# A decoder trunk on one core: gate and up in two passes over a chunk, and the matrices moved to multiples of 512 bytes

## The chip, the cores and the metric

The kernel runs on one core of a Trainium2 chip. The metric is the time of one execution on the device in microseconds (us), smaller is better. All times below are of the kernel before the change, and the trace is of one execution of it.

## What is computed

Two layers of a decoder trunk on a sequence of 256 positions and a width of 1024, all in float32. Each layer has a mixer part and a feed-forward part:

```
for l in range(DEPTH):                      # 2 layers
    h = rms_norm(x, attn_norm[l])
    proj = h @ w_in[l]                      # retention, sparse attention and gMLP heads
    mix = concatenate([retention(...), nsa(...), spatial_gating(...)])
    x = x + mix @ w_out[l]
    h = rms_norm(x, ffn_norm[l])
    gate, up = split(h @ w_gate_up[l], 2)   # 1024 -> 2 x 2816
    x = x + (silu(gate) * up) @ w_down[l]   # 2816 -> 1024
```

## The kernel before

**Three products for one.** Every matrix that meets a weight is split into a high and a low part, both of type float32r: the weights into `whi` and `wlo`, the activations into `hh` and `hl` (side by side in one tile, `hcat`, seen whole as `hx`). A product is then hh·whi + hl·whi + hh·wlo.

**The stream of weights.** The weights come in pieces of at most 128 x 1024 floats. A piece lands in one of three staging tiles `wst` (a DMA from SyncE's queue), ScalarE casts it to one of six tiles `whi` (CAST), VectorE subtracts to one of six tiles `wlo` (TENSOR_TENSOR). A staging tile comes free when its low part is made; `done` gives `whi` and `wlo` back when the piece has been used. `split_hi[i]` and `ready[i]` are the events that say that the high and the low part of piece i exist.

**Three ways of multiplying.** A matmul has a stationary operand, 128 columns that are loaded into TensorE, and a moving one that streams past it.
- `project` (the mixer's input chunks and the first chunk of gate and up): the activation is stationary, the weights move. A chunk is 8 blocks of the inner dimension (k) x 2 row tiles x 3 products = 48 matmuls. Per layer five mixer chunks and the first chunk of gate and up have 512 columns, one has 384 and one, `nv`, has 274.
- `project_t` (the other ten chunks of gate and up in each layer): the weights are stationary, the activations move. Per chunk 8 k x 4 column groups, each with a wide matmul of 512 columns (whi with hh and hl together) and a narrow one of 256 (wlo with hh). The four results are in four PSUM banks, two of `acc` and two of `sm`.
- `residual` (the output projection with 8 k, the down projection with 22): the activation is stationary (`ah`, `al`, `nsh`, `rth`, ...), the weights move, 4 parts x 3 products of 512 columns per k. In the very last call one of the four parts is cut into two of 256 columns.

**What sets the order.** A planner (`Desk.run`) with costs of its own writes out one fixed order for each engine when the program is built; on the chip an engine takes its instructions in that order and waits for semaphores. Nearly every instruction is issued from one line of a helper, L201, so the rows below are told apart by the tiles' names.

**Where the tiles lie.** Tiles are laid one behind the other in a partition's memory, each in whole slots of 32 bytes. The first tile of the kernel starts at byte 16512, which is 128 past a multiple of 512. All tiles up to `hcat` have sizes that are multiples of 512 bytes, so `wst`, `whi`, `wlo`, `x` and `hcat` all start 128 past. Then come tiles of odd sizes, so that the pools opened later (`ah`, `al`, `nsh`, `nsl`, `gmh`, `gml`, `rth`, `rtl`, `Q`, `Kh`, `Kl`) start 288 past a multiple of 512. A stationary operand of 128 float32r columns takes 512 bytes in a partition.

Of the kernel before, what the change touches and what calls it, by code (L numbers as in the profile page):

```python
# [10 lines left out]
F32R = mybir.dt.float32r  # L11
# [6 lines left out]
T = 256  # L18
# [133 lines left out]

START = [(0, 0), (1, 0), "w", "w", (0, 1), (1, 1), "w", "w"]

NR, NREP = 33, 3
# [238 lines left out]
class Trunk:  # L396
    def __init__(self, ctx, tc, x, wts, cst, oh, relb, par, w1, w2, wsT, out):
        self.ctx, self.tc, self.nc = ctx, tc, tc.nc
        nc = self.nc
        self.d = dict(x=x, wts=wts, cst=cst, oh=oh, relb=relb, par=par, w1=w1, w2=w2, wsT=wsT, out=out)  # L400
        self.PE, self.V = Engine("PE", nc.tensor), Engine("DVE", nc.vector)
        self.A, self.G = Engine("ACT", nc.scalar), Engine("POOL", nc.gpsimd)
        self.SP, self.GQ = Engine("DMA", nc.sync), Engine("SWDMA", nc.gpsimd)

        def preload(table):
            if table == "lnexp":
                nc.scalar.preload_act_table_set("natural_log_exp_and_others")

        self.desk = Desk(preload)
        self.keep = ctx.enter_context(tc.tile_pool(name="keep", bufs=1))  # L410
        psum = ctx.enter_context(tc.tile_pool(name="psum", bufs=1, space=bass.MemoryType.PSUM))
        bank = lambda n: psum.tile([128, 512], F32, tag=n, name=n)
        self.acc = Pool([bank(f"acc{i}") for i in range(4)])
        self.sm = Pool([bank(f"sm{i}") for i in range(4)])
        self.norms = 0
        self.wst = Pool([self.fixed(f"wst{i}", [128, 1024]) for i in range(3)])
        self.whi = Pool([self.fixed(f"whi{i}", [128, 1024], F32R) for i in range(6)])
        self.wlo = Pool([self.fixed(f"wlo{i}", [128, 1024], F32R) for i in range(6)])
        self.w2k = Pool([self.fixed(f"w2k{i}", [128, 512]) for i in range(6)])
# [12 lines left out]
        self.extra = []  # L432

    def fixed(self, name, shape, dt=F32):
        return self.keep.tile(shape, dt, tag=name, name=name)

    def tiny(self, name, shape, dt=F32):
        if name not in self.tinies:
# [74 lines left out]
    def weights(self, i, a):  # L513
        return self.part(self.hi, i, a), self.part(self.lo, i, a)

    def done(self, i):
        self.desk.give(self.whi, self.hi.pop(i))
        self.desk.give(self.wlo, self.lo.pop(i))

    def mm3(self, ps, a, w, first, last):  # L520

# [5 lines left out]

    def setup(self):
        nc = self.nc
        c = self.fixed("cst", [128, C_W])  # L530
        self.cst = c
        self.ident = c[:, C_ID : C_ID + 128]
        self.tri = c[:, C_TRI : C_TRI + 128]
        self.rowvalid = c[:, C_RV : C_RV + 1]
        self.vmask = c[:96, C_VM : C_VM + 6]
        self.dec = c[:, C_DEC:].rearrange("p (h n) -> p h n", h=6)
        self.kc = self.fixed("kc", [128, 2, 2, 16], F32R)
        self.B = self.fixed("B", [128, 6, 256])
        self.Bc = self.fixed("Bc", [128, 2, 3, 2, 16])
        self.par = self.fixed("par", [128, P_W])  # L540
        self.qg = self.fixed("qg", [128, 1])
        self.wsT = self.fixed("wsT", [128, 4, 128])
        self.w1 = self.fixed("w1", [128, 2, 16, 64])
        self.w2 = self.fixed("w2", [128, 64])
        self.ev_cst, self.ev_bias, self.ev_scr = Event(), Event(), Event()
        self.ev_par = [Event() for _ in range(L)]
        self.ev_lay = [Event() for _ in range(L)]
        self.ev_cmp = [Event() for _ in range(L)]
        self.ev_dec = Event()
        self.ev_w = [Event() for s in START if s == "w"]  # L550
        self.ev_sent = [Event() for s in START if s == "w"]
        self.ev_x = [[Event(), Event()] for _ in range(2)]
# [459 lines left out]
    def compress(self, l):  # L1012
# [43 lines left out]

        pk = yield Need(self.sm)
        yield PE.matmul(pk[:32, :64], hk, self.w2[:64, :], start=True, stop=True)
        sq, ss = tiny("csq", [32, 64]), tiny("css", [32, 1])
        yield A.activation(sq, pk[:32, :64], AF.Square, accum_out=ss)  # L1060
        yield V.tensor_scalar(ss, ss, 1.0 / 64, EPS, op0=ALU.mult, op1=ALU.add)
        r = yield from self.rsqrt(ss, "crs")
        kd = tiny("kd", [32, 2, 64])
        yield [V.tensor_scalar_mul(kd[:, i, :], pk[:32, :64], r) for i in range(2)]
        give(self.sm, pk)
        pt = yield Need(self.sm)
# [319 lines left out]
    def mix_open(self, l):  # L1386
        pool = self.tc.tile_pool(name=f"mix{l}", bufs=1, reuse_waits="tile")
        mix = pool.__enter__()

        def tl(name, shape, dt=F32):  # L1390
            return mix.tile(shape, dt, tag=name, name=f"{name}_{l}")

        self.gmh, self.gml = tl("gmh", [128, 2, 256], F32R), tl("gml", [128, 2, 256], F32R)
        self.nsh = [tl(f"nsh{j}", [128, 256], F32R) for j in range(3)]
        self.nsl = [tl(f"nsl{j}", [128, 256], F32R) for j in range(3)]
        self.rth, self.rtl = tl("rth", [128, 3, 256], F32R), tl("rtl", [128, 3, 256], F32R)
        self.Q = tl("Q", [128, 6, 256], F32R)
        self.Kh, self.Kl = (tl(k, [128, 2, 2, 256], F32R) for k in ("Kh", "Kl"))
        self.aT = tl("aT", [128, 2, 272])
# [7 lines left out]
        self.S = Pool([tl(f"S{i}", [128, 512]) for i in range(NS)])  # L1407
        pair = lambda: [Event(), Event()]
# [79 lines left out]
    def project_t(self, pieces, then):  # L1488


        mm = self.PE.matmul
        ps = []
        for j in range(4):
            p = yield Need(self.acc if j < 2 else self.sm)
            ps.append(p)
        for i in pieces:
            yield self.ready[i]
            for a in range(2):
                k = 2 * (i - pieces[0]) + a
                for t in range(2):  # L1500
                    yield self.hready[t][k]
                wh, wl = self.weights(i, a)
                cols = [slice(j * 128, j * 128 + 128) for j in range(4)]
                last = k == KD - 1
                wide = [
                    mm(ps[j], wh[:, s], self.hx[:, k].rearrange("p r n -> p (r n)"), start=k == 0, stop=last, lat=False)
                    for j, s in enumerate(cols)
                ]
                low = [
                    mm(ps[j][:, :T], wl[:, s], self.hh[:, k, :], start=False, stop=False, lat=False)  # L1510
                    for j, s in enumerate(cols)
                ]
                for op in low + wide if last else wide + low:
                    yield op
            self.done(i)
        self.desk.after = self.desk.LAT["PE"]
        then(ps)
        self.desk.after = 0
# [127 lines left out]
    def main(self):  # L1646
# [13 lines left out]
        for l in range(L):  # L1660
# [50 lines left out]
                after = self.store  # L1711
            yield from self.residual(l, idx("down")[0], KF, 3, 4, acted, True, after, l + 1 == L)
            pool.__exit__(None, None, None)


def trunk_kernel(tc, *args):
# [51 lines left out]
```

## Time and profile before

| | |
|---|---|
| median of 3 runs | 637.78 us (637.48 to 637.89) |
| the profiled execution's own time | 638.01 us |
| its span in the trace | 636.2 us (1.8 us lie around it) |
| TensorE (PE) matmuls, busy | 630.5 us |
| VectorE (DVE) busy | 448.5 us |
| ScalarE (ACT) busy | 365.8 us |
| DMA traffic | 111.63 MB, mean 175 GB/s |
| granted TensorE clock | 1.0, the 2.4 GHz level, in all 40 slices |

A row of the trace gives a matmul a duration that runs from its start to the modelled end of its result, so durations of neighbouring matmuls overlap. What a matmul costs is the distance from its start to the start of the next one; it is read from the start column of the timeline.

### The profile page before, as it was taken

How to read it: one execution, taken by the hardware profiler on the slowest of the kernel's cores; microseconds unless marked ns; L12 is line 12 of the kernel's file. 1: busy time of each engine (PE TensorE's matmuls, PEld its weight loads, DVE VectorE, ACT ScalarE, POOL GpSimd, SP SyncE). 2: the span in 40 equal slices, each digit the busy share in tenths (PEclk: the TensorE clock that was granted, in tenths of full speed). 3: DMA queues.
4: the chain of work that ended last, by engine and by line, in shares of the span. 5: the costliest groups of instructions: out<-in, count | busy, mean ns of one | idle time of the engine just before them, and what ended most of it. 6: DMA issues, size and time to landing. Idle time of an engine off the chain costs nothing.

```text
span 636.2 us, 9911 instructions
## 1 busy us (share of the span) xinstructions
PE 630.5 (99%) x3638; PEld 534.7 (84%) x3638; DVE 448.5 (70%) x970; ACT 365.8 (57%) x679; POOL 10.7 (2%) x25
## 2 busy tenths in 40 slices
PE   8999999999999999999999999999999999999997
PEld 6888788888888888888888988888888888888886
DVE  4989996586667767654488898866857767766432
ACT  5869844675555555543377795546755555555330
POOL 1120000000000000100000000000000000000000
PEclk9999999999999999999999999999999999999999
DMA  8974153356555555575436522625565555565631
GB/s 308 305 270 161 31 178 124 114 185 214 187 191 186 183 198 183 189 266 193 133 134 227 176 90 71 203 100 165 189 199 181 193 195 171 191 196 173 201 101 66
DMA packets 33600, 111.63 MB, mean 175 GB/s; under 512 B 4291, under 2 KB 5571, under 8 KB 33552
## 3 DMA queue, kind: packets, MB, share of 16 engines
q1 hardware_dynamic: 33232, 110.62, 52.8%
q8 instruction: 28, 0.46, 0.3%
q0 software_dynamic: 176, 0.36, 0.1%
q14 instruction: 20, 0.16, 0.1%
q10 hardware_dynamic: 144, 0.03, 0.0%
HBM read 109.64 MB, written 1.35 MB: 174 GB/s over the span
## 4 chain that ended last, share of the span: by engine, by line
PE 98%; DMA 1%; DVE 0%; SPq 0%; issue 0%; ACT 0%
PE acc L201 69%; PE sm L201 29%; DMA wst<-in_wts_dram 1%; SPq L201 0%; DVE S L201 0%; DVE x L201 0%; ACT hcat L201 0%; DVE amx L201 0%; ACT whi L201 0%
## 5 line engine op out<-in xcount | busy, mean ns | idle before, releaser
L201 DVE TENSOR_TENSOR wlo<-wst,whi 128x1024 fp32r<-128x1024 f32 (+3 forms) x196 | 234.0, 1197 | 131.6 <-ACT whi L201 130.6
L201 ACT CAST whi<-wst 128x1024 fp32r<-128x1024 f32 (+3 forms) x196 | 200.7, 1028 | 183.7 <-PE sm L201 49.6
L201 PE MATMUL acc<-whi,hcat 128*128 128x512 f32 (+2 forms) x512 | 139.4, 379 | 0.3 <-ACT hcat L201 0.3
L201 PEld LDWEIGHTS acc<-whi,hcat 128*128 128x128 f32 x512 | 91.0, 188 | 15.3 <-ACT whi L201 0.6
L201 PE MATMUL acc<-hcat,whi 128*128 128x512 f32 x320 | 101.2, 396 | 0.0
L201 PE MATMUL sm<-hcat,whi 128*128 128x512 f32 x320 | 99.7, 392 | 0.0
L201 PE MATMUL acc<-wlo,hcat 128*128 128x512 f32 (+2 forms) x256 | 79.5, 378 | 0.0
L201 PEld LDWEIGHTS sm<-hcat,whi 128*128 128x128 f32 x320 | 59.9, 188 | 14.2
L201 PEld LDWEIGHTS acc<-hcat,wlo 128*128 128x128 f32 x320 | 58.8, 188 | 11.8
L201 PE MATMUL sm<-hcat,wlo 128*128 128x256 f32 x320 | 64.0, 281 | 0.0
L201 PE MATMUL acc<-hcat,wlo 128*128 128x256 f32 x320 | 63.8, 281 | 0.0
L201 PEld LDWEIGHTS acc<-hcat,whi 128*128 128x128 f32 x320 | 50.9, 190 | 1.7
L201 PEld LDWEIGHTS acc<-wlo,hcat 128*128 128x128 f32 x256 | 46.4, 188 | 6.9
L201 PE MATMUL acc<-whi,ah 128*128 128x512 f32 (+1 forms) x176 | 50.7, 382 | 0.0
L201 PE MATMUL acc<-whi,al 128*128 128x512 f32 (+1 forms) x176 | 50.6, 381 | 0.0
L201 PE MATMUL acc<-wlo,ah 128*128 128x512 f32 (+1 forms) x176 | 50.4, 380 | 0.0
L201 PEld LDWEIGHTS sm<-hcat,wlo 128*128 128x128 f32 x320 | 49.5, 190 | 0.0
L201 PEld LDWEIGHTS acc<-whi,al 128*128 128x128 f32 x176 | 31.8, 188 | 6.2
L201 PEld LDWEIGHTS acc<-wlo,ah 128*128 128x128 f32 x176 | 31.8, 188 | 6.2
L201 PEld LDWEIGHTS acc<-whi,ah 128*128 128x128 f32 x176 | 31.9, 188 | 6.1
L201 ACT ACTIVATE hcat<-sm,par 128x128 fp32r<-128x128 f32 (+1 forms) x56 | 17.3, 393 | 10.1 <-PE sm L201 9.8
L201 DVE SCALAR_TENSOR_TENSOR hcat<-sm,par,hcat 128x128 fp32r<-128x128 f32 (+1 forms) x56 | 17.4, 362 | 6.0 <-ACT hcat L201 6.0
(213 smaller groups left out, 732.6 us busy)
## 6 DMA issues: line engine op xcount, KB each, us to landing
wst<-in_wts_dram SPq DMA_DIRECT2D x179, 512.0 KB, 3.5
PT<-in_wts_dram SPq DMA_DIRECT2D x7, 512.0 KB, 7.6
wst<-in_wts_dram SPq DMA_DIRECT2D x8, 384.0 KB, 3.1
w<-in_w_dram SPq DMA_DIRECT2D x4, 512.0 KB, 7.7
wst<-in_wts_dram SPq DMA_DIRECT2D x3, 411.0 KB, 4.1
x<-in_x_dram SPq DMA_DIRECT2D x4, 256.0 KB, 5.0
wst<-in_wts_dram SPq DMA_DIRECT2D x4, 256.0 KB, 4.1
B<-scr SPq DMA_DIRECT2D x4, 192.0 KB, 3.7
```

The costliest lines, as they stand in the source:

```text
L201: return Op(self.name, lambda: fn(*a, **k), dur, table, lat, prio, banks)
```

## The change

`project_t` goes over a chunk twice: first all wide products with `whi` (it waits for `split_hi` of a piece), then all narrow products with `wlo` (it waits for `ready`). `done` is cut in two: a high part goes back to its pool once its wide products are issued and its low part exists, a low part once its narrow products are issued. All other code paths issue the same operations as before.

The second part moves tiles. A tile `pad` ahead of `wst` (384 bytes) makes the first matrix start at byte 16896, a multiple of 512; the tiles made in `setup` are put in an order in which the large ones keep to multiples of 512; a second pad does the same for the pools of each layer; `aT`, whose size is no multiple of 512, goes behind the others. `csq`, a small scratch tile, is dropped and `kd` used in its place. In the built program `wst`, `whi`, `wlo`, `x`, `hcat`, `ah`, `al`, `nsh`, `nsl`, `gmh`, `gml`, `rth`, `rtl`, `Q`, `Kh`, `Kl` all start at a multiple of 512. No tile changes its size or its type.

```
+FIRST, SLOT, GRAIN = 16512, 32, 512
...
+        self.kept = 0
+        self.pad(FIRST)
         self.wst = Pool([self.fixed(f"wst{i}", [128, 1024]) for i in range(3)])
...
     def fixed(self, name, shape, dt=F32):
+        size = 4
+        for n in shape[1:]:
+            size *= n
+        self.kept += -(-size // SLOT) * SLOT
         return self.keep.tile(shape, dt, tag=name, name=name)
+
+    def pad(self, first):
+        gap = -(first + self.kept) % GRAIN
+        if gap:
+            self.fixed(f"pad{self.kept}", [128, gap // 4])
...
+    def done_hi(self, i):
+        def release():
+            yield self.ready[i]
+            self.desk.give(self.whi, self.hi.pop(i))
+        self.desk.fork(release())
+
+    def done_lo(self, i):
+        self.desk.give(self.wlo, self.lo.pop(i))
...
     def project_t(self, pieces, then):
...
-        for i in pieces:
-            yield self.ready[i]
-            for a in range(2):
-                k = 2 * (i - pieces[0]) + a
-                for t in range(2):
-                    yield self.hready[t][k]
-                wh, wl = self.weights(i, a)
-                cols = [slice(j * 128, j * 128 + 128) for j in range(4)]
-                last = k == KD - 1
-                wide = [
-                    mm(ps[j], wh[:, s], self.hx[:, k].rearrange("p r n -> p (r n)"), start=k == 0, stop=last, lat=False)
-                    for j, s in enumerate(cols)
-                ]
-                low = [
-                    mm(ps[j][:, :T], wl[:, s], self.hh[:, k, :], start=False, stop=False, lat=False)
-                    for j, s in enumerate(cols)
-                ]
-                for op in low + wide if last else wide + low:
-                    yield op
-            self.done(i)
+        cols = [slice(j * 128, j * 128 + 128) for j in range(4)]
+        for i in pieces:
+            yield self.split_hi[i]
+            for a in range(2):
+                k = 2 * (i - pieces[0]) + a
+                for t in range(2):
+                    yield self.hready[t][k]
+                wh = self.part(self.hi, i, a)
+                for j, s in enumerate(cols):
+                    yield mm(
+                        ps[j], wh[:, s], self.hx[:, k].rearrange("p r n -> p (r n)"), start=k == 0, stop=False, lat=False
+                    )
+            self.done_hi(i)
         for i in pieces:
             yield self.ready[i]
             for a in range(2):
                 k = 2 * (i - pieces[0]) + a
+                wl = self.part(self.lo, i, a)
+                for j, s in enumerate(cols):
+                    yield mm(ps[j][:, :T], wl[:, s], self.hh[:, k, :], start=False, stop=k == KD - 1, lat=False)
+            self.done_lo(i)
...
+        self.pad(FIRST)
```

In the program before, TensorE has in a chunk of gate and up, at its first k (`acc` and `sm` are PSUM banks, `hcat` the moving activations, `whi` and `wlo` the stationary weights; the last number is the columns that move):

```order
L201 MATMUL acc_63<-hcat,whi_75 128x512
L201 MATMUL acc_64<-hcat,whi_75 128x512
L201 MATMUL sm_68<-hcat,whi_75 128x512
L201 MATMUL sm_67<-hcat,whi_75 128x512
L201 MATMUL acc_63<-hcat,wlo_81 128x256
L201 MATMUL acc_64<-hcat,wlo_81 128x256
L201 MATMUL sm_68<-hcat,wlo_81 128x256
L201 MATMUL sm_67<-hcat,wlo_81 128x256
```

Wide and narrow change every four matmuls, eight times in a chunk. In the changed program the one place in a chunk where they change, at the last k of the wide ones and the first of the narrow ones:

```order
L203 MATMUL acc_63<-hcat,whi_78 128x512
L203 MATMUL acc_64<-hcat,whi_78 128x512
L203 MATMUL sm_68<-hcat,whi_78 128x512
L203 MATMUL sm_67<-hcat,whi_78 128x512
L203 MATMUL acc_63<-hcat,wlo_81 128x256
L203 MATMUL acc_64<-hcat,wlo_81 128x256
L203 MATMUL sm_68<-hcat,wlo_81 128x256
L203 MATMUL sm_67<-hcat,wlo_81 128x256
```

Here 32 wide matmuls stand ahead of this place and 32 narrow ones from it on; the order of the k and of the column groups is as before.

VectorE makes the low parts and takes in the results of a chunk (`w2k<-acc`, `w2k<-sm`, the product with `rbc`, the product of gate and up, `al`). Before, around the end of one chunk:

```order
L201 TENSOR_TENSOR wlo_83<-wst_72,whi_77 128x1024
L201 TENSOR_TENSOR w2k_87<-acc_63,w2k_87 128x256
L201 TENSOR_TENSOR wlo_84<-wst_73,whi_78 128x1024
L201 TENSOR_TENSOR w2k_87<-acc_64,w2k_87 128x256
L201 TENSOR_TENSOR w2k_87<-w2k_87,rbc_1486 128x512
L201 TENSOR_TENSOR wlo_85<-wst_71,whi_79 128x1024
L201 TENSOR_TENSOR w2k_89<-sm_68,w2k_89 128x256
L201 TENSOR_TENSOR wlo_80<-wst_72,whi_74 128x1024
L201 TENSOR_TENSOR w2k_89<-sm_67,w2k_89 128x256
L201 TENSOR_TENSOR w2k_89<-w2k_89,w2k_87 128x512
L201 TENSOR_TENSOR wlo_81<-wst_73,whi_75 128x1024
```

In the changed program, around the end of one chunk:

```order
L203 TENSOR_TENSOR wlo_82<-wst_74,whi_76 128x1024
L203 TENSOR_TENSOR wlo_83<-wst_72,whi_77 128x1024
L203 TENSOR_TENSOR w2k_88<-acc_63,w2k_88 128x256
L203 TENSOR_TENSOR w2k_88<-acc_64,w2k_88 128x256
L203 TENSOR_TENSOR w2k_88<-w2k_88,rbc_1486 128x512
L203 TENSOR_TENSOR wlo_84<-wst_73,whi_78 128x1024
L203 TENSOR_TENSOR w2k_90<-sm_68,w2k_90 128x256
L203 TENSOR_TENSOR w2k_90<-sm_67,w2k_90 128x256
L203 TENSOR_TENSOR w2k_90<-w2k_90,w2k_88 128x512
L203 TENSOR_TENSOR wlo_85<-wst_74,whi_79 128x1024
L203 TENSOR_TENSOR al_3_1478<-w2k_90,ah_3_1467 128x512
```

The subtractions stood one by one between the additions; now the two additions of a pair stand together, and per chunk it is still four subtractions beside the same seven other operations. ScalarE's order changes in the same way within the chunks of gate and up; outside them the orders of VectorE, ScalarE and TensorE are the same as before.

## Rows read from the trace of the kernel before

**Rows 1.** The page: busy time of the engines, the granted clock, and the chain that ended last.

```profile
PE 630.5 (99%) x3638; PEld 534.7 (84%) x3638; DVE 448.5 (70%) x970; ACT 365.8 (57%) x679; POOL 10.7 (2%) x25
...
PEclk9999999999999999999999999999999999999999
...
PE 98%; DMA 1%; DVE 0%; SPq 0%; issue 0%; ACT 0%
```

**Rows 2.** What TensorE waited for in the whole span: us in total, times, longest.

```profile
PE sm L201 <- DVE w2k L201: 1.4, 1, 1.4
PE sm L201 <- DMA x<-in_x_dram: 0.5, 1, 0.5
PE acc L201 <- ACT hcat L201: 0.3, 1, 0.3
PE sm L201 <- DVE amx L201: 0.2, 1, 0.2
```

**Rows 3.** Timeline of TensorE in a mixer chunk of `project`, 512 columns, stationary `hcat` (128 past a multiple of 512): start, length of the merged row, instruction, count.

```profile
36.06 1.07 PE L201 MATMUL acc<-whi,hcat 128*128 128x512 f32 x4
36.97 0.62 PE L201 MATMUL acc<-wlo,hcat 128*128 128x512 f32 x2
37.42 1.07 PE L201 MATMUL acc<-whi,hcat 128*128 128x512 f32 x4
38.33 0.62 PE L201 MATMUL acc<-wlo,hcat 128*128 128x512 f32 x2
38.78 1.07 PE L201 MATMUL acc<-whi,hcat 128*128 128x512 f32 x4
```

**Rows 4.** The same view in the down projection of the first layer, 512 columns, stationary `ah` and `al` (288 past a multiple of 512).

```profile
302.74 1.09 PE L201 MATMUL acc<-wlo,ah 128*128 128x512 f32 x4
303.67 1.09 PE L201 MATMUL acc<-whi,al 128*128 128x512 f32 x4
304.60 1.10 PE L201 MATMUL acc<-whi,ah 128*128 128x512 f32 x4
305.54 1.09 PE L201 MATMUL acc<-wlo,ah 128*128 128x512 f32 x4
```

**Rows 5.** The same view in `project_t`, one chunk of gate and up from its start (203.74) to the start of the next (214.95); stationary `whi` and `wlo` (128 past). Rows of two stand in turn on `acc` and `sm`; those left out are the second pair of a four, and from 213.06 to 214.02 eight narrow ones follow each other.

```profile
203.74 0.62 PE L201 MATMUL acc<-hcat,whi 128*128 128x512 f32 x2
...
204.65 0.40 PE L201 MATMUL acc<-hcat,wlo 128*128 128x256 f32 x2
204.88 0.40 PE L201 MATMUL sm<-hcat,wlo 128*128 128x256 f32 x2
205.12 0.63 PE L201 MATMUL acc<-hcat,whi 128*128 128x512 f32 x2
...
206.05 0.40 PE L201 MATMUL acc<-hcat,wlo 128*128 128x256 f32 x2
...
206.52 0.63 PE L201 MATMUL acc<-hcat,whi 128*128 128x512 f32 x2
...
213.06 0.40 PE L201 MATMUL acc<-hcat,wlo 128*128 128x256 f32 x2
...
214.02 0.63 PE L201 MATMUL acc<-hcat,whi 128*128 128x512 f32 x2
...
214.95 0.62 PE L201 MATMUL acc<-hcat,whi 128*128 128x512 f32 x2
```

**Rows 6.** The same view in the last half bank of the last call of `residual`, 256 columns, stationary `ah` and `al` (288 past); 20 matmuls from the first row to the last.

```profile
630.03 0.28 PE L201 MATMUL acc<-wlo,ah 128*128 128x256 f32 x1
...
632.43 0.28 PE L201 MATMUL sm<-whi,ah 128*128 128x256 f32 x1
```

**Rows 7.** The same view in the mixer chunk `nv`, 274 columns; from one k to the next the moving weights start 1096 bytes further on. Two rows are one k.

```profile
47.27 0.66 PE L201 MATMUL acc<-whi,hcat 128*128 128x274 f32 x4
47.77 0.41 PE L201 MATMUL acc<-wlo,hcat 128*128 128x274 f32 x2
48.03 0.67 PE L201 MATMUL acc<-whi,hcat 128*128 128x274 f32 x4
...
49.01 0.67 PE L201 MATMUL acc<-whi,hcat 128*128 128x274 f32 x4
49.51 0.41 PE L201 MATMUL acc<-wlo,hcat 128*128 128x274 f32 x2
49.77 0.41 PE L201 MATMUL acc<-whi,hcat 128*128 128x274 f32 x2
```

**Rows 8.** Busy time of each engine by stretch (us, and instructions): a mixer, gate and up of the first layer, its down projection.

```profile
46.00:112.00 66.00, 65.77 (x525) 56.05 (x524) 56.99 (x216) 44.72 (x111) 0.00 (x0) 1.00 0.41 130
157.00:259.00 102.00, 102.00 (x586) 89.42 (x585) 73.06 (x98) 56.36 (x89) 0.00 (x0) 1.00 0.57 190
259.00:320.00 61.00, 61.00 (x268) 49.15 (x267) 31.18 (x38) 25.41 (x38) 2.18 (x3) 1.00 0.56 187
```

(The columns are: stretch, its length, PE, PEld, DVE, ACT, POOL, granted clock, DMA share, GB/s.)

**Rows 9.** The two splits of a weight piece, and the DMA that brings it (KB, us from issue to landing).

```profile
L201 DVE TENSOR_TENSOR wlo<-wst,whi 128x1024 fp32r<-128x1024 f32 x179 | 219.3, 1228 | 122.0 <-ACT whi L201 121.1 <-issue 0.6
L201 ACT CAST whi<-wst 128x1024 fp32r<-128x1024 f32 x179 | 187.7, 1053 | 173.0 <-PE sm L201 49.6 <-issue 46.1 <-PE acc L201 31.6
...
wst<-in_wts_dram SPq DMA_DIRECT2D x179, 512.0 KB, 3.5
```

More of the change, by code (lines that the diff above doesn't have):

```diff
@@ L514, in weights @@
         return self.part(self.hi, i, a), self.part(self.lo, i, a)
+    def done_hi(self, i):
[5 more added lines that the diff above has]
+        self.desk.give(self.wlo, self.lo.pop(i))
     def done(self, i):
-        self.desk.give(self.whi, self.hi.pop(i))
-        self.desk.give(self.wlo, self.lo.pop(i))
+        self.done_hi(i)
+        self.done_lo(i)
     def mm3(self, ps, a, w, first, last):
@@ L529, in setup @@
         nc = self.nc
+        self.B = self.fixed("B", [128, 6, 256])
+        self.wsT = self.fixed("wsT", [128, 4, 128])
+        self.w1 = self.fixed("w1", [128, 2, 16, 64])
+        self.kc = self.fixed("kc", [128, 2, 2, 16], F32R)
+        self.Bc = self.fixed("Bc", [128, 2, 3, 2, 16])
         c = self.fixed("cst", [128, C_W])
@@ L536, in setup @@
         self.dec = c[:, C_DEC:].rearrange("p (h n) -> p h n", h=6)
-        self.kc = self.fixed("kc", [128, 2, 2, 16], F32R)
-        self.B = self.fixed("B", [128, 6, 256])
-        self.Bc = self.fixed("Bc", [128, 2, 3, 2, 16])
         self.par = self.fixed("par", [128, P_W])
         self.qg = self.fixed("qg", [128, 1])
-        self.wsT = self.fixed("wsT", [128, 4, 128])
-        self.w1 = self.fixed("w1", [128, 2, 16, 64])
         self.w2 = self.fixed("w2", [128, 64])
@@ L1058, in compress @@
         yield PE.matmul(pk[:32, :64], hk, self.w2[:64, :], start=True, stop=True)
-        sq, ss = tiny("csq", [32, 64]), tiny("css", [32, 1])
-        yield A.activation(sq, pk[:32, :64], AF.Square, accum_out=ss)
+        kd, ss = tiny("kd", [32, 2, 64]), tiny("css", [32, 1])
+        yield A.activation(kd[:, 0, :], pk[:32, :64], AF.Square, accum_out=ss)
         yield V.tensor_scalar(ss, ss, 1.0 / 64, EPS, op0=ALU.mult, op1=ALU.add)
         r = yield from self.rsqrt(ss, "crs")
-        kd = tiny("kd", [32, 2, 64])
         yield [V.tensor_scalar_mul(kd[:, i, :], pk[:32, :64], r) for i in range(2)]
@@ L1398, in mix_open @@
         self.Kh, self.Kl = (tl(k, [128, 2, 2, 256], F32R) for k in ("Kh", "Kl"))
-        self.aT = tl("aT", [128, 2, 272])
         self.Vt = [tl(f"V{t}", [128, 256]) for t in range(2)]
@@ L1407, in mix_open @@
         self.S = Pool([tl(f"S{i}", [128, 512]) for i in range(NS)])
+        self.aT = tl("aT", [128, 2, 272])
         pair = lambda: [Event(), Event()]
@@ L1495, in project_t @@
             ps.append(p)
+        cols = [slice(j * 128, j * 128 + 128) for j in range(4)]
[10 more added lines that the diff above has]
+                    )
+            self.done_hi(i)
         for i in pieces:
@@ L1499, in project_t @@
                 k = 2 * (i - pieces[0]) + a
-                for t in range(2):
-                    yield self.hready[t][k]
-                wh, wl = self.weights(i, a)
-                cols = [slice(j * 128, j * 128 + 128) for j in range(4)]
-                last = k == KD - 1
-                wide = [
-                    mm(ps[j], wh[:, s], self.hx[:, k].rearrange("p r n -> p (r n)"), start=k == 0, stop=last, lat=False)
-                    for j, s in enumerate(cols)
-                ]
-                low = [
-                    mm(ps[j][:, :T], wl[:, s], self.hh[:, k, :], start=False, stop=False, lat=False)
-                    for j, s in enumerate(cols)
-                ]
-                for op in low + wide if last else wide + low:
-                    yield op
-            self.done(i)
+                wl = self.part(self.lo, i, a)
+                for j, s in enumerate(cols):
+                    yield mm(ps[j][:, :T], wl[:, s], self.hh[:, k, :], start=False, stop=k == KD - 1, lat=False)
+            self.done_lo(i)
         self.desk.after = self.desk.LAT["PE"]
```

## The prediction

> **What bounds the kernel now.** I read the page first. The chain that ended last is TensorE for 98% of the span, TensorE has a matmul in flight for 630.5 of 636.2 us, and its clock is granted at 1.0, the 2.4 GHz level, in every slice [rows 1]. Then I asked what TensorE waited for: 2.4 us in all, in four single waits [rows 2]. So no engine and no transfer keeps it waiting, and the time can only fall if TensorE's own matmuls follow each other faster. The third view is therefore the timeline of TensorE, for the distance between starts. At 2.4 GHz 512 columns take 213.3 ns and 256 take 106.7 ns; whatever a matmul costs above its columns I call its surplus.
>
> In a mixer chunk twelve matmuls of 512 columns go from 36.06 to 38.78 us, 226.7 ns each: a surplus of 13.3 ns [rows 3]. In the down projection twelve go from 302.74 to 305.54 us, 233.3 ns each: a surplus of 20.0 ns [rows 4]. The columns, the types and the clock are the same; the stationary operand starts 128 bytes past a multiple of 512 in the first and 288 past in the second. In gate and up a four of wide ones that follows narrow ones takes 0.93 us, 232.5 ns each (surplus 19.2), the four at a chunk's start 0.91 us, 227.5 ns each; a four of narrow ones takes 0.47 us, 117.5 ns each (surplus 10.8), and eight in a row take 0.96 us, 120.0 ns each (surplus 13.3). A chunk takes 214.95 - 203.74 = 11.21 us [rows 5]. Narrow ones with a stationary operand 288 past run at 120.0 ns too, 20 in 2.40 us [rows 6]. And the moving operand's start does not matter as far as the trace shows: in `nv` it differs by 72 bytes from one k to the next (1096 = 2 x 512 + 72), and the six matmuls of a k take 0.76 us, 126.7 ns each, at 47.27 as at 49.01 (surplus 12.5 over 274 / 2.4 = 114.2) [rows 7].
>
> So there is a surplus of about 13 ns per matmul, whatever the column count, which rises to 20 for wide ones in the residual and for wide ones that alternate with narrow ones. The change touches both: the order, and where the stationary operand starts.
>
> **The order of gate and up, alone.** Nothing is added: 32 wide and 32 narrow matmuls per chunk before and after. Only the changes of width go, from sixteen to two per chunk. If wide ones in a row run as in rows 3 and narrow ones as the eight in rows 5, a chunk takes 32 x (226.7 + 120.0) = 11.09 us, 0.12 less; 20 chunks (ten per layer) save 2.3 us. If the wide ones stay at 232.5 ns, because here the stationary operand changes four times on one moving operand, a chunk takes 32 x (232.5 + 120.0) = 11.28 us and 20 chunks lose 1.4 us. I take the gain: the four at a chunk's start already run at 227.5 ns [rows 5].
>
> What hides the new order's demands: the narrow half now begins 32 x 0.227 = 7.3 us after the wide half, so low parts are wanted later, but their six tiles also come free only in the narrow half. Four tiles are in use, two hold pieces of the next chunk. The third piece of the next chunk can be subtracted once the first narrow piece is done, some 8.2 us into this chunk, and is wanted in the next chunk's narrow half, 11 us later; the subtraction takes 1.23 us, the cast 1.05, the transfer 3.5 [rows 9]. VectorE is busy 73.06 of 102.00 us in this stretch and ScalarE 56.36 [rows 8], which is 8.0 and 6.2 us of a chunk of 11.21. They have room, and I cost the waits at nothing. SyncE's queue issues the same transfers in the same order, four per chunk.
>
> **The place of the operands.** Adding a pad and moving tiles adds no instruction that computes. What a stationary operand at a multiple of 512 costs is nowhere in this trace, so I bound it. One end: 128 past is already as good as 0, and the surplus stays 13.3 ns. The other end: the whole surplus comes from the start and it falls to nothing. Between them: from 288 to 128 the wide surplus falls by 6.7 ns in 160 bytes; carried on in a straight line over the last 128 bytes it falls by another 5.3, to 8.0 ns. That is an estimate from two points. The row nearest to it is the pair of narrow ones from 204.65 to 204.88, 115 ns each, a surplus of 8.3 [rows 5]: so a matmul can go that close to its columns even now. I take 8.0 ns: 221.3 ns wide, 114.7 narrow.
>
> [...]
>
> **The sum**, against the profiled execution's own 638.0 us (span 636.2 and 1.8 around it; the median of the runs, 637.78, is 0.2 below):
> - gate and up: 32 x (221.3 + 114.7) = 10.75 us a chunk, 0.46 less than 11.21, times 20: 9.2 us (2.3 of them from the order alone).
> - residual: 8 + 22 k, 4 parts, 3 products, 2 layers are 720 wide matmuls; the last call's cut part turns 66 of them into 132 narrow ones. 654 x 12.0 ns = 7.8 us, and 132 x 5.3 ns = 0.7 us.
> - project: 8 chunks (seven of the mixer, one of gate and up) x 48 x 2 layers = 768 matmuls x 5.3 ns = 4.1 us. This is the softest term: in the mixer VectorE is busy 56.99 of 66.00 us [rows 8], and part of the gain may come back as a wait for it.
>
> Together 21.8 us: 616 us. With the whole surplus gone it would be 19.4 + 13.1 + 1.8 + 10.2 = 44.5 us, 593.5 us. This is the outer bound.
>
> **Rivals.**
> 1. *128 past was already good.* Then only the residual gains, 654 x 6.7 ns = 4.4 us, and the order 2.3: 631.3 us. For it: two points do not make a line, and a step between 128 and 288 explains rows 3 and 4 as well; the narrow rows show no difference between 128 and 288 at all (120.0 in both) [rows 5, 6]. Against it: the 8.3 ns pair, which shows that 13.3 is not a floor.
> 2. *The place does not matter.* The residual's 233.3 ns would then come from its order: its weights alternate between two column halves under one stationary operand, where `project` keeps the weights and alternates the stationary one. Then only gate and up's order counts, between 2.3 us saved and 1.4 lost: 635.7 to 639.4, middle 637.5 us. [...]
> 3. *Slower: low parts come late.* The narrow half waits at its first piece because the subtraction was held up behind the additions that wait for the chunk before. One subtraction of 1.23 us laid bare per chunk costs 20 x 1.23 = 24.6 us, 616 + 24.6 = 640.7 us. It decides against the kernel from (638 - 616) / 20 = 1.1 us a chunk. For it: low tiles are freed in bursts, and the order now lets two additions go ahead. Against it: the 11 us of lead and VectorE's 8.0 us of work in a chunk of 10.75.
>
> **How the numbers follow.** Likeliest, 0.48: the surplus falls well below 13 ns; its own range is 599 to 625 us, from nearly all of it gone to about half of the 21.8 us. Rival 1: 0.32. Rival 2: 0.13. Rival 3: 0.05. Something else: 0.02. The range has to hold the first two, 599 to 633 us, which leaves out about 2 in 10. A measurement of this kernel can tell a change from none at about 0.2%, 1.3 us. Faster: 0.48 + 0.32 + a third of rival 2 = 0.84. The same: 0.07. Slower: rival 3, a third of rival 2, 0.09.
>
> **What would show it.** In the changed kernel's timeline, distances between starts. Mixer chunk: 221 ns says my line holds, 226.7 says rival 1. Down projection: 221 ns mine, 226.7 rival 1, 233.3 rival 2. Gate and up: 32 wide ones at one distance and 32 narrow ones at 115 ns, a chunk in 10.75 us; 11.09 us says that only the order worked; wide ones still at 232.5 say that even it did not. What TensorE waits for must stay at some 2 to 3 us; a wait for `wlo` or `whi` there, twenty times over, is rival 3, and waits in the mixer for VectorE eat the third term. The prediction is wrong if the distances are not even within a group, so that a surplus belongs to something that neither the order nor the place sets.

## The result and the profile after

The changed kernel takes 633.3 us (median of 4 runs, 632.6 to 634.73), the kernel before beside it 637.84 us (4 runs, 637.48 to 638.22): a ratio of 0.9932, 95% interval 0.9913 to 0.995. It is faster by 4.5 us, where 21.8 were forecast. The profiled execution has a time of 634.73 us and a span of 633.0.

The page of the changed kernel: busy time, granted clock, chain that ended last; then what TensorE waited for. They answer [rows 1] and [rows 2].

```profile
PE 627.0 (99%) x3638; PEld 536.4 (85%) x3638; DVE 446.7 (71%) x970; ACT 367.1 (58%) x679; POOL 11.3 (2%) x25
...
PEclk9999999999999999999999999999999999999999
...
PE 98%; DMA 1%; DVE 0%; SPq 0%; issue 0%
```

```profile
PE sm L203 <- DVE w2k L203: 1.4, 1, 1.4
PE sm L203 <- DMA x<-in_x_dram: 1.0, 1, 1.0
PE sm L203 <- DVE amx L203: 0.2, 1, 0.2
```

The bound is as before: TensorE's own matmuls, at a granted clock of 1.0 over the whole span, 2.6 us of waits, none for `whi` or `wlo`. So what changed is the distance between starts. The timeline of TensorE in the changed kernel, in the mixer chunk of [rows 3] and in the first down projection of [rows 4] (start, length of the merged row, instruction, count):

```profile
36.48 1.07 PE L203 MATMUL acc<-whi,hcat 128*128 128x512 f32 x4
37.38 0.62 PE L203 MATMUL acc<-wlo,hcat 128*128 128x512 f32 x2
37.84 1.07 PE L203 MATMUL acc<-whi,hcat 128*128 128x512 f32 x4
38.74 0.62 PE L203 MATMUL acc<-wlo,hcat 128*128 128x512 f32 x2
```

```profile
301.86 1.07 PE L203 MATMUL acc<-wlo,ah 128*128 128x512 f32 x4
302.77 1.07 PE L203 MATMUL acc<-whi,al 128*128 128x512 f32 x4
303.68 1.07 PE L203 MATMUL acc<-whi,ah 128*128 128x512 f32 x4
304.58 1.07 PE L203 MATMUL acc<-wlo,ah 128*128 128x512 f32 x4
```

Ten matmuls from 36.48 to 38.74 are 226 ns each, the mixer's old 226.7 within the rounding of the view. Twelve from 301.86 to 304.58 are 226.7 ns each, where [rows 4] had 233.3. So the residual came down to the mixer's pace, and the mixer did not move. One chunk of gate and up, as in [rows 5]:

```profile
204.56 0.63 PE L203 MATMUL acc<-hcat,whi 128*128 128x512 f32 x2
...
205.49 0.62 PE L203 MATMUL acc<-hcat,whi 128*128 128x512 f32 x2
...
208.22 0.62 PE L203 MATMUL acc<-hcat,whi 128*128 128x512 f32 x2
...
211.84 0.40 PE L203 MATMUL acc<-hcat,wlo 128*128 128x256 f32 x2
...
215.67 0.63 PE L203 MATMUL acc<-hcat,whi 128*128 128x512 f32 x2
```

32 wide take 7.28 us, 227.5 ns each: the first four 232.5, the sixteen from 208.22 on 226.3. 32 narrow take 3.83 us, 119.7 ns each. The chunk is 11.11 us, 0.10 less than before.

The whole trace by stage, each from the start of its first `project`, `residual` or gate-and-up matmul to the first of the next stage (us; all from starts in the timelines; the three kernels to the right are those of the experiments):

| stage | before | after | order alone | place alone | last call 192 past |
|---|---|---|---|---|---|
| two mixers | 201.03 | 201.05 | 201.62 | 200.94 | 200.93 |
| two output projections | 49.78 | 48.89 | 49.77 | 49.19 | 49.07 |
| gate and up, both layers | 248.86 | 246.92 | 246.95 | 248.83 | 246.92 |
| first down projection | 62.91 | 61.31 | 62.90 | 61.28 | 61.27 |
| second down projection | 61.76 | 61.29 | 61.75 | 61.26 | 60.29 |
| sum | 624.34 | 619.46 | 622.99 | 621.50 | 618.48 |

The stages give 4.9 us back. The profiled execution shows only 638.01 - 634.73 = 3.3, because its head was 1.6 us longer. The start of the timeline, of the kernel before and of the changed one:

```profile
6.11 0.55 PE L201 MATMUL sm<-cst,x 128*128 128x128 f32 x3 [0.48 <-DMA x<-in_x_dram]
...
8.34 0.72 PE L201 MATMUL acc<-whi,hcat 128*128 128x512 f32 x2 [0.34 <-ACT hcat L201]
```

```profile
6.86 0.90 PE L203 MATMUL sm<-cst,x 128*128 128x128 f32 x3 [1.00 <-DMA x<-in_x_dram]
...
9.97 0.88 PE L203 MATMUL acc<-whi,hcat 128*128 128x512 f32 x2
```

The first wide matmul starts at 9.97 instead of 8.34. In the other profiled executions of this study, with the same work ahead of it, it starts anywhere from 7.56 to 9.81 us, so I count the head as belonging to the execution and not to the change; no run shows what sets it.

### The profile page after: what moved, and what is told of

Read it like the earlier page. It is cut to its first block, busy times and chain, and to the rows that moved or that the text cites. A ratio compares the mean times of both kernels' runs of the same rounds, so it can differ in the third digit from the quotient of the medians.

```text
span 633.0 us, 9872 instructions
## 1 busy us (share of the span) xinstructions
PE 627.0 (99%) x3638; PEld 536.4 (85%) x3638; DVE 446.7 (71%) x970; ACT 367.1 (58%) x679; POOL 11.3 (2%) x25
## 4 chain that ended last, share of the span: by engine, by line
PE 98%; DMA 1%; DVE 0%; SPq 0%; issue 0%
PE acc L203 68%; PE sm L203 30%; DMA x<-in_x_dram 1%; SPq L203 0%; DVE S L203 0%; DVE x L203 0%; DVE amx L203 0%
## 5 line engine op out<-in xcount | busy, mean ns | idle before, releaser
L203 PE MATMUL acc<-hcat,whi 128*128 128x512 f32 x320 | 99.3, 391 | 0.0
L203 PEld LDWEIGHTS acc<-hcat,whi 128*128 128x128 f32 x320 | 58.9, 188 | 11.2
L203 PEld LDWEIGHTS acc<-hcat,wlo 128*128 128x128 f32 x320 | 51.2, 191 | 1.6
L203 DVE TENSOR_TENSOR w2k<-sm,w2k 128x256 f32<-128x256 f32 x40 | 16.9, 423 | 42.6 <-ACT w2k L203 42.6
```

What stands on the lines that cost most here:

```text
L203: return Op(self.name, lambda: fn(*a, **k), dur, table, lat, prio, banks)
```

## Experiments

Each run's text speaks of theories that came up on the way. A: what counts is where the stationary operand itself starts (a multiple of 64 or of 512 is good). B: the new order pays only together with the new places. C: what counts is the distance between the starts of the stationary and the moving operand. D: C, but only distances of 64 bytes and more cost. C256: C, modulo 256. E: neither, the whole layout does it.

**The order alone.** The kernel before with the new `project_t` and `done`, no pad and no tile moved. Against the changed kernel:

```
-        self.pad(FIRST)
         self.wst = Pool([self.fixed(f"wst{i}", [128, 1024]) for i in range(3)])
...
-        self.B = self.fixed("B", [128, 6, 256])
...
-        self.pad(FIRST)
```

> Only the order of gate and up is changed; every tile lies where it lay before (stationary operands 128 past a multiple of 512 in project and project_t, 288 past in the residual). Theory A (a stationary operand at a multiple of 64 bytes is as good as one at a multiple of 512; only one off a multiple of 64 costs more): a chunk of gate and up in 11.1 us as in the changed kernel, the residual's wide matmuls stay at 233.3 ns, the whole gains 1.9 us: 635.9. Theory B (the order only pays together with the new places): the wide ones of gate and up stay near 232 ns, a chunk takes 11.3 us, no gain: 637.8 to 639.

Measured: 635.82 us (12 runs) against 637.94 (23 runs), ratio 0.9973 (0.9962 to 0.9984). Gate and up has the changed kernel's length, 246.95 us for both layers, and the other stages keep the length of before, but for the first mixer (0.6 us more, at its start, where TensorE waited 2.0 us for `x` and the granted clock showed 0.50 from 8 to 11 us). The order pays 1.9 us by itself, without the places; B falls.

**The places alone.** The changed kernel with the `project_t` and `done` of before:

```
-            yield self.split_hi[i]
+            yield self.ready[i]
...
+                for op in low + wide if last else wide + low:
+                    yield op
+            self.done(i)
```

> Only the tiles are moved to multiples of 512; gate and up keep the old order. Theory A: residual wide matmuls 226.7 ns, a chunk of gate and up 11.2 us as before, wide ones after narrow ones still 232.5 ns; gain 2.5 to 3 us, 635.2. Theory B: gate and up gains too, wide ones after narrow ones at 227 ns, a chunk in 11.05 us: 632.

Measured: 634.84 us (6 runs), ratio 0.9963 (0.9948 to 0.9977). The residual is at 226.7 ns as in the changed kernel, gate and up as before, 248.83 us. In the stages the places give 624.34 - 621.50 = 2.8 us and the order 1.9 (gate and up), together the 4.9 of the changed kernel within 0.2.

**Only the pools moved.** The kernel with the places alone, without its first pad, so that the stationary `ah`, `al` start at a multiple of 512 while the weights stay 128 past. By a slip it has the old order of gate and up as well, which its expectation does not say; it is compared with the kernel before, in the residual.

```
-        self.pad(FIRST)
         self.wst = Pool([self.fixed(f"wst{i}", [128, 1024]) for i in range(3)])
```

> As the changed kernel, but without the pad ahead of the first tile: the weights and hcat start 128 past a multiple of 512 as before, the pools of each layer at a multiple of 512. In the residual the moving operand is 128 past and the stationary one at 0. Theory A (only the stationary operand's own place counts): residual wide 226.7 ns, the whole as the changed kernel, 633.3. Theory C (the two operands must start at the same distance from a multiple of 512; they did in project before, did not in the residual before, and do everywhere in the changed kernel): residual wide at 233.3 ns, 636.

Measured: 637.89 us (10 runs), ratio 1.0 (0.9991 to 1.0009). The timeline in its first down projection:

```profile
302.90 1.09 PE L203 MATMUL acc<-whi,al 128*128 128x512 f32 x4
303.82 1.10 PE L203 MATMUL acc<-whi,ah 128*128 128x512 f32 x4
304.76 1.09 PE L203 MATMUL acc<-wlo,ah 128*128 128x512 f32 x4
305.69 1.08 PE L203 MATMUL acc<-whi,al 128*128 128x512 f32 x4
```

Twelve in 2.79 us, 232.5 ns each: a stationary operand at a multiple of 512 runs no better than the one 288 past in [rows 4]. A falls for the residual. The moving weights still start 128 past, so the two starts differ.

**Everything 32 past.** The changed kernel with both pads made 32 bytes longer: equal starts, but not at multiples of 64.

```
-        gap = -(first + self.kept) % GRAIN
+        gap = -(first + self.kept - 32) % GRAIN
```

> As the changed kernel, but every matrix starts 32 past a multiple of 512. Theory A: the stationary operand is off a multiple of 64 everywhere, so wide matmuls take 233.3 ns in the residual (+3 us), in project (576 x 6.7 ns = +3.8 us) and in project_t (640 x 6.7 ns = +4.3 us); narrow ones stay at 120.0; 633.3 + 11 = 644. Theory C (same distance is enough): all wide ones at 226.7 ns, 633.3.

Measured: 633.17 us (4 runs), ratio 0.993 (0.9917 to 0.9943), the changed kernel's time. Its down projection:

```profile
300.34 1.07 PE L203 MATMUL acc<-whi,al 128*128 128x512 f32 x4
301.24 1.07 PE L203 MATMUL acc<-whi,ah 128*128 128x512 f32 x4
302.15 1.07 PE L203 MATMUL acc<-wlo,ah 128*128 128x512 f32 x4
303.06 0.84 PE L203 MATMUL acc<-whi,al 128*128 128x512 f32 x3
```

Twelve in 2.72 us, 226.7 ns each. The multiple of 512 is not needed; equal starts are. A falls altogether, C stands.

**Three distances.** The changed kernel with `hcat` moved by 32, 256 and 64 bytes and the later pools by 128, 192 and 320, the weights at multiples of 512. Here the first of them; the others have 64 and 16 floats and 192 and 320 bytes.

```
+        self.fixed("shift", [128, 8])
         self.hx = self.fixed("hcat", [128, KD, 2, T], F32R)
...
-        self.pad(FIRST)
+        self.pad(FIRST - 128)
```

> The changed kernel with hcat 32 past a multiple of 512 and each layer's pools 128 past; the weights stay at multiples of 512. Stationary less moving start is then 32 bytes in project, -32 in project_t, 128 in the residual. Theory C (the distance between the two starts counts, not the place of either): wide matmuls above 226.7 ns where the distance matters; if any distance does, 232 to 233.3 ns in all three and a chunk of gate and up in 11.28 us. Theory D (only a distance of 64 or more matters): project and project_t at 226.7, the residual at 232 to 233. Theory A (the stationary's own place, a multiple of 64) was refuted by the kernel with everything 32 past.

> hcat 256 past a multiple of 512, pools 192 past, weights at multiples of 512: distance 256 (and -256) in project and project_t, 192 in the residual. If the distance counts in steps of 256: project and project_t at 226.7, a chunk of gate and up in 11.1 us. If only 512 is free of cost: 232 to 233.3 in both. Residual 232 to 233.3 in either case.

> hcat 64 past a multiple of 512, pools 320 past, weights at multiples of 512: distance 64 (and -64) in project and project_t, 320 in the residual. Theory C: 232 to 233.3 ns in all three. Theory D's other half (a distance of up to 64 is free): 226.7 in project and project_t, 232 to 233.3 in the residual.

Measured, one run each: 638.92, 632.86 and 635.51 us. The down projections of the three, at distances of 128, 192 and 320:

```profile
300.01 1.08 PE L203 MATMUL acc<-wlo,ah 128*128 128x512 f32 x4
300.94 1.10 PE L203 MATMUL acc<-whi,al 128*128 128x512 f32 x4
301.87 1.09 PE L203 MATMUL acc<-whi,ah 128*128 128x512 f32 x4
302.80 1.10 PE L203 MATMUL acc<-wlo,ah 128*128 128x512 f32 x4
```

```profile
299.63 1.07 PE L203 MATMUL acc<-whi,ah 128*128 128x512 f32 x4
...
305.13 1.07 PE L203 MATMUL acc<-whi,ah 128*128 128x512 f32 x4
```

```profile
301.34 1.10 PE L203 MATMUL acc<-wlo,ah 128*128 128x512 f32 x4
...
304.14 0.63 PE L203 MATMUL acc<-wlo,ah 128*128 128x512 f32 x2
```

These are 12 in 2.79 us (232.5 ns), 24 in 5.50 us (229.2 ns) and 12 in 2.80 us (233.3 ns). The mixers of the first two, with `hcat` 32 and 256 past, six matmuls from row to row (those between are left out):

```profile
35.83 1.09 PE L203 MATMUL acc<-whi,hcat 128*128 128x512 f32 x4
...
37.23 1.09 PE L203 MATMUL acc<-whi,hcat 128*128 128x512 f32 x4
```

```profile
35.99 1.07 PE L203 MATMUL acc<-whi,hcat 128*128 128x512 f32 x4
...
37.35 1.07 PE L203 MATMUL acc<-whi,hcat 128*128 128x512 f32 x4
```

32 past they take 233.3 ns each, 256 past the 226.7 of equal starts; 64 past they take 233.3 too (six from 35.76 to 37.16). D falls, since 32 already costs all of it. And 256 being as good as 0 (226.7 both), and 320 as bad as 64 (233.3 both), speaks for a count modulo 256.

All this is for 512 columns. The mixer chunk of 384 columns does not show it. Six of its matmuls in the changed kernel, and six with `hcat` 32 past:

```profile
104.94 0.86 PE L203 MATMUL acc<-whi,hcat 128*128 128x384 f32 x4
...
105.99 0.86 PE L203 MATMUL acc<-whi,hcat 128*128 128x384 f32 x4
```

```profile
103.43 0.86 PE L203 MATMUL acc<-whi,hcat 128*128 128x384 f32 x4
...
104.47 0.86 PE L203 MATMUL acc<-whi,hcat 128*128 128x384 f32 x4
```

175.0 ns with equal starts and 173.3 with a distance of 32.

**Residual sorted by width.** The last call of the residual alternates three wide and two narrow matmuls under each stationary operand. Here a step issues its wide ones first; nothing else differs from the changed kernel.

```
-            for op in sum(ops, []):
+            for op in sorted(sum(ops, []), key=lambda op: -op.dur):
```

> The changed kernel, and in every step of the residual all wide matmuls are issued ahead of the narrow ones; that differs only in the last call, where a step has nine wide and six narrow ones and the width now changes twice a step and not six times. If the change of width is what keeps the wide ones of that call at 235 ns: they run at about 230 ns over the nine, its 15 steps and the head save 0.5 to 0.8 us, 632.6. If not: no difference from the changed kernel, 633.3.

Measured: 632.3 us (4 runs). The runs of the kernel before beside it spread from 637.48 to 639.91, so the ratio of 0.9897 (0.9873 to 0.9922) flatters it; by the trace the last call takes 60.95 us against 61.29, 0.34 less, where 0.5 to 0.8 were expected.

**Many distances in one execution.** The twelve weight tiles 32 bytes longer each. The text says that `hcat` stays; in the built program it did not, the twelve times 32 bytes put it 128 past a multiple of 256, and the distances below are counted with that.

```
-        self.whi = Pool([self.fixed(f"whi{i}", [128, 1024], F32R) for i in range(6)])
-        self.wlo = Pool([self.fixed(f"wlo{i}", [128, 1024], F32R) for i in range(6)])
+        self.whi = Pool([self.fixed(f"whi{i}", [128, 1032], F32R) for i in range(6)])
+        self.wlo = Pool([self.fixed(f"wlo{i}", [128, 1032], F32R) for i in range(6)])
```

> The changed kernel, but the six tiles of the weights' high part and the six of the low part are each 32 bytes longer, so that they no longer start at one place: the high tiles start 0, 32, 64, 96, 128 and 160 bytes past a multiple of 256, the low ones 192, 224, 0, 32, 64 and 96. hcat and the stage's pools stay at multiples of 256. So one execution holds many distances between the stationary and the moving operand, and each piece of weights runs at the distance of its tile. The runs so far gave for 512 columns, by the distance (stationary start minus moving start) modulo 512: 0 and 256: 226.7 ns; 192 and 448: 228.9 ns; 32, 64, 128, 160, 320, 384, 480: 232 to 233.3 ns. Theory C256 (only the distance modulo 256 counts): pieces in one kernel will run at their own pace, 226.7 at 0, 228.9 at 192 (and so in project where the weights start 64 past, because there they are the moving operand), 232.5 to 233.3 at 32, 64, 128, 160 and 224 wherever the tile lies. Theory E (it is a property of the whole layout, such as which tiles lie beside each other, and the pace by distance is a coincidence): all pieces of a stage run at one pace. For 256 columns the runs so far gave 120.0 ns at 0 and 256, 116.7 at 480 and 115.5 at 448: C256 expects the low tile that starts 192 past to give 115.5, the one 224 past 116.7, the one at 0 120.0, and leaves 32, 64 and 96 open. Time: between 633 and 638 us, no verdict is sought.

Measured: 638.14 us (one run). Mean distance between starts in gate and up, each piece's first two matmuls and its last left out, and four of some 318 ns at a distance of 32 (60 to 70 matmuls a cell), beside what the kernels with one distance per stage showed:

| distance modulo 256 | 0 | 32 | 64 | 96 | 128 | 160 | 192 | 224 |
|---|---|---|---|---|---|---|---|---|
| 512 columns, this run (ns) | 229.0 | 233.7 | - | - | 233.8 | 232.6 | 228.8 | 233.6 |
| 512 columns, other runs (ns) | 226.7 | 233.3 | 233.3 | - | 232.5 | 233.3 | 228.9 | 233.4 |
| 256 columns, this run (ns) | - | - | 113.5 | 120.0 | 118.4 | 117.6 | 115.7 | 117.3 |

Pieces of one kernel run at their own pace, and for wide matmuls it fits the other runs' within 1.3 ns at every distance but 0, so E falls for them. At 0 the mean hides two cases: pieces that follow a wide piece are at 226 to 227 ns at once, pieces that follow narrow matmuls take between 224 and 236 ns a matmul, 230.5 on average over their eight.

**The low part 64 past.** The table's best cell for narrow matmuls, 113.5 ns, put to use: `wlo` alone 64 bytes past (a second pad after it puts `hcat` back; `GRAIN` is 256 to make room).

```
+        self.fixed("shift", [128, 16])
         self.wlo = Pool([self.fixed(f"wlo{i}", [128, 1024], F32R) for i in range(6)])
+        self.fixed("back", [128, 48])
```

> The changed kernel with one difference: the six tiles of the weights' low part start 64 bytes past a multiple of 256 (320 past a multiple of 512); everything else stays at multiples of 256. In gate and up's narrow half the stationary operand then starts 64 past the moving one; in project and in the residual, where the low part is the moving operand, the distance is -64, the same as 192 modulo 256. Theory C256 with the prices of the map by distance (256 columns: 120.0 ns at 0, 113.5 at 64; 512 columns: 226.7 at 0, 228.9 at 192): 20 chunks x 32 narrow x 6.5 ns = 4.2 us saved, 256 wide of project x 2.2 ns = 0.6 us lost, 218 wide of the residual x 2.2 ns = 0.5 us lost: 3.1 us below the changed kernel, 630.2 us, 0.988 of the kernel before. The narrow half of a chunk then goes at 113.5 ns, a chunk in 10.9 to 11.0 us. Theory E (the map's pace at 64 came from its mixture of places): no difference, 633.3 us.

> As the run with the low part's tiles 64 bytes past a multiple of 256, and with the residual's matmuls of a step sorted by width (wide before narrow), which differs in the last call alone. C256: the last call saves 0.3 us in its own part, as the grouped kernel's trace against the changed kernel's, so 629.9 us, 0.9875 of the kernel before. Theory E: as the grouped kernel, 632.3 to 633 us.

Measured: both 634.92 us (6 runs each), ratios 0.9947 (0.9931 to 0.9963) and 0.9949 (0.9935 to 0.9963). Neither C256's 630 nor E's 633: slower than the changed kernel by 1.6 us. By stage, the first of the two against the changed kernel: gate and up 1.1 us less instead of 4.2, mixers 0.9 more, output projections 0.5, down projections 1.3 more. The sorting that the second adds did not shorten its last call (61.68 us against 61.54). Two prices were read wrongly. The narrow ones went at 3.77 us for 32, 117.8 ns, in every chunk, where the map's pieces at the same distance had gone at 113.5. So distance alone does not set their pace. The run with `hcat` 64 past, where the narrow ones are at the negative of this distance, 192 modulo 256, shows it within one program: its chunks take one of two paces. Its timeline, at the start of the narrow half of two neighbouring chunks:

```profile
155.50 0.40 PE L203 MATMUL acc<-hcat,wlo 128*128 128x256 f32 x2
...
156.21 0.40 PE L203 MATMUL sm<-hcat,wlo 128*128 128x256 f32 x2
...
166.60 0.39 PE L203 MATMUL acc<-hcat,wlo 128*128 128x256 f32 x2
...
167.28 0.39 PE L203 MATMUL sm<-hcat,wlo 128*128 128x256 f32 x2
```

Six in 0.71 us, 118.3 ns, and six in 0.68, 113.3 ns, at the same distance in one program; each chunk keeps its pace to the end, and the two paces take turns from chunk to chunk. The PSUM banks, which also take turns, do not decide it: the banks whose chunks run at 118 in the first layer have 113 in the second. And in the residual the distance now changes every few matmuls (`whi` at 0, `wlo` at 192), which costs more than either distance. The down projection with `wlo` 64 past:

```profile
305.08 1.09 PE L203 MATMUL acc<-whi,al 128*128 128x512 f32 x4
...
307.85 1.09 PE L203 MATMUL acc<-whi,al 128*128 128x512 f32 x4
```

A round of twelve takes 2.77 us, 230.8 ns each; 8 at 226.7 and 4 at 228.9 would be 227.4.

**The last call 192 past.** The changed kernel with `ah` and `al` of the last layer alone moved.

```
+            if l + 1 == L:
+                ffn.tile([128, 48], F32, tag="shift", name="shift")
             ah = [ffn.tile([128, 2, 256], F32R, tag=f"ah{c}", name=f"ah{l}_{c}") for c in range(NCH)]
```

> The changed kernel with one difference: in the last layer the tiles of the down projection's stationary operand start 192 bytes past a multiple of 512, everything else stays at multiples of 512. This is the one call whose steps alternate three wide and two narrow matmuls. In the run with the pools 192 past and hcat 256 past, this stage took 60.33 us against 61.29 in the changed kernel: a wide matmul averaged 549 cycles and a narrow one 272 in an alternating step, against 562 and 275. Theory C256 (pace follows the distance modulo 256 and what ran just before): this stage alone gets shorter, to 60.3 us, everything else stays, the time is 633.3 - 1.0 = 632.3 us, 0.9915 of the kernel before. Theory E (the pace belongs to the whole layout): the stage stays at 61.3 us and the time at 633.3, 0.993.

Measured: 631.92 us (6 runs, 631.41 to 634.17) against 637.98 (11 runs), ratio 0.9904 (0.9886 to 0.9923): the lowest median of all kernels here, though the runs of the sorted residual, 632.22 to 633.01, lie within its spread. Its last call takes 60.29 us, 1.0 less than in the changed kernel, the other stages agree within 0.2. One cut step (nine wide, six narrow) in the changed kernel and in this one, from the first row to the last:

```profile
600.61 0.28 PE L203 MATMUL sm<-wlo,ah 128*128 128x256 f32 x1
...
603.41 0.28 PE L203 MATMUL sm<-wlo,ah 128*128 128x256 f32 x1
```

```profile
600.53 0.28 PE L203 MATMUL sm<-wlo,ah 128*128 128x256 f32 x1
...
603.27 0.28 PE L203 MATMUL sm<-wlo,ah 128*128 128x256 f32 x1
```

2.80 against 2.74 us. Where these widths alternate, 192 is better than 0; where all have 512 columns, it is worse (229.2 against 226.7). Other distances do not help the last call: in the runs above it took 61.41 us at 64, 61.90 at 128 and 61.76 at 160, against 61.29 at 0.

## Why the prediction was wrong, point by point

- **The bound** held: a granted clock of 1.0 in all 40 slices, waits of 2.6 us, and all of the gain in distances between starts.
- **The surplus** counts 106.7 ns for 256 columns and 213.3 for 512. What the rows show of that is a difference: at equal starts 512 columns settle at 226.7 ns [rows 3] and 256 in a row at 120.0 [rows 5], so 256 columns more cost 106.7. That the first 256 cost as much, with a surplus of 13.3 on top, is the author's estimate; the 175.0 ns of 384 columns lie near the 173.3 that it gives.
- **The place, the step that failed.** 19.5 of the 21.8 us came from it, and it gave 3.0. The straight line from 288 and 128 to "8.0 ns at 0" took the stationary operand's own start for the cause. Its start is not the cause: at 0 with the weights 128 past it ran at 232.5 ns, at 32 with the weights 32 past at 226.7. What counts for 512 columns is the distance between the two starts, modulo 256: 226.7 ns at distances of 0 and 256, 228.9 at 192, 232.5 to 233.4 at 32, 64, 128, 160 and 224, whatever the two operands' own places. By what mechanism, no run shows. Before the change that distance was already 0 in `project` and in gate and up (both operands 128 past) and 160 in the residual; after it is 0 everywhere. So the place term was 0 for `project` (4.1 forecast; mixers 201.03 before, 201.05 after) and 0 for gate and up (6.9 of its 9.2), and 13.3 ns is the wide surplus at the best distance that any run showed. The rows at hand left room for it as a rival: [rows 3] and [rows 4] differ in the distance between the two operands as much as in the stationary start.
- **"The moving operand's start does not matter"**, from the equal pace of the k of `nv` [rows 7], was the wrong lesson from the one group where the distance varies: the two k that were compared lie at distances of 184 and 0 and take 126.7 ns both, but what 274 columns do not show, 512 columns do (226.7 ns at 0, 233.3 at 32).
- **The 8.3 ns pair** [rows 5] was taken as a sign that 13.3 is no floor. It was a narrow pair just after wide ones; narrow ones in a row stay at 119.7 in the changed kernel. For narrow ones in a row 13.3 is indeed no floor, but not at equal starts: at a distance of 192 they reached 113.3, a surplus of 6.6. For wide ones no run shows a settled pace below the mixer's.
- **The order term**, 2.3 us forecast, is 1.9: wide ones 227.5 instead of 226.7, because the first four after the narrow half still take 232.5. Its sign and its reason, the changes of width, hold.
- **The residual**, 8.5 us in the sum, gave 0.9 + 1.6 + 0.5 = 3.0. 6.7 ns for each of 654 would have been 4.4. The 264 of the first down projection came near it (1.6 of 1.8), the 192 of the output projections less so (0.9 of 1.3). The last call alternates widths and gave 0.5 of 1.3: while they alternate, its wide ones average 232.5 ns before and 234.6 after, and the gain lies in the narrow ones among them (119.5 to 115.3) and in the wide ones at the call's two ends (233.5 to 228.0).
- **The hiding of the low parts** held: no wait for `wlo` or `whi`. Rival 3 did not happen.
- **The rivals.** Rival 1, "128 past was already good", came closest (6.7 us forecast against 4.5; its signs for the mixer and the down projection, 226.7 ns in both, came true) but has the wrong reason: 128 past was good only because the moving operand was 128 past as well (with the weights at 0, a stationary operand 128 past ran at 232.5 ns). Rival 2 fell with the residual. The range ended at 633, 0.3 below the median; that it came so near is owed to rival 1, which it had to hold, and not to the line.

## What to carry to other kernels

Where a new stationary operand is loaded for every matmul of 512 float32r columns, look at the difference of the two start addresses, not at either address: make it one value in a whole stage, 0 modulo 256 where all matmuls have 512 columns (226.7 ns here, against 228.9 to 233.4 at the other distances tried), and measure another where widths alternate (here 192, with a last call of 60.29 us against 61.29 at 0). Do not carry the 0 over to other widths: 384 columns gained nothing by it (175.0 ns at 0, 173.3 at 32), and 256 columns in a row took 120.0 ns at 0, more than the 113 to 118 at 64, 192 and 224. Keep equal widths and equal distances together: a round that mixed the distances 0 and 192 took 230.8 ns a matmul, more than either by itself (226.7 and 228.9), and the first wide ones after narrow ones took 232.5 instead of 226.7. And before a line is drawn through two points, list everything in which the two rows differ.

## What was not expected of the hardware

- Pace by distance between the starts of stationary and moving operand, modulo 256, 512 float32r columns: 226.7 ns at 0, 228.9 at 192, 232.5 to 233.4 at 32, 64, 128, 160 and 224.
- 256 columns in a row take 120.0 ns at 0. At 64 and 192 two paces were seen: at 192 some 118 and 113 ns in turns, chunk by chunk, in one program; at 64 113.5 in one program and 117.8 in another. What picks the one or the other is open; the attempt to use the faster one failed.
- 384 columns take 175.0 ns at 0 and 173.3 at 32: the cost of unequal starts at 512 columns (226.7 against 233.3 at 32) is not there.
- After a change of width at distance 0 the first four wide matmuls take 232.5 ns, and 226.3 ns is reached some eight matmuls in; the first eight average 230.0 (1.84 us in the chunk shown).
- Why 256, and why 192 (228.9 ns) is nearly as good as 0 (226.7) while 64 is as bad as 160 (233.3 both), was not settled.
